# Waits on a pool's former bytes tile by tile, a bias copy from DRAM to DRAM, and the last tile's three pieces in three PSUM tiles

## The chip, the cores and the metric

The kernel runs on one core of one Trainium2 chip. The metric is the device time of one execution in microseconds (us), median of the runs shown; lower is better. The core's engines each have an instruction stream of their own: TensorE (PE; the loading of its weights is PEld), VectorE (DVE), ScalarE (ACT), GpSimd (POOL) and SyncE (SP). SP, ACT and POOL also issue DMAs. An engine works in the order of its stream, so an instruction that waits holds back all that stand behind it.

## The reference

One decoder layer for a prompt of 1024 tokens and a sample group of 8 × 8 tokens with 512 past tokens each:

```python
h = rms_norm(x, norm_mix);  z = h @ w_in          # q, three K/V branches, gates, 512 pooling channels
o_att  = nsa(q, gates, kv_cmp, kv_sel, kv_win)    # compressed, selected and window branch, per-head gates,
                                                  # all with a relative-position bias from rel_bias
o_pool = pool_mix(u)                              # trailing means over 2/4/8/16 positions minus the token,
                                                  # a linear map per group, a scale per channel
x = x + concat(o_att, o_pool) @ w_out
x = x + swiglu(rms_norm(x, norm_ffn));  y = rms_norm(x, norm_final)
```

All of it is in 32-bit floating point. The new cache rows are outputs too.

## The kernel before, in words

A product of two fp32 operands is made of three PE products: each operand is split into a high and a low part (`split`: ACT makes the high part as a cast, L163, DVE the low part as a difference, L164).

The stages, by the profile's time. Up to about 118 us: the norm, the first projection of 128-column units (`useq`), the four pooling units (`pool_unit`, `pool_mm`), the bias tables (`prep_bias`) and the gates. A unit's weight is loaded by SP into `wraw` (L210) and split two units ahead. To about 260 us: the other units (the next one after the pooling units is that of column 512), the compressed branch. To 650 us: attention, tile by tile, with the output projection as filling work. To 715: the entry of the feed-forward part. To 1151: its first product by a scheme of block sums (`pq`, L1405). To 1353 its second, and then `last_group`, which adds the last part of the second product to nine token tiles (eight of 128 rows, the sample tile of 64), and takes the final norm.

The order of instructions on an engine is found by a scheduler in the tile framework, from the program's text and its dependences; it is not written out by hand. Buffers come from pools. A pool opened where another was closed takes over bytes of the former one, and its first instructions wait for the former users.

`prep_bias` makes with two matmuls a table `bt` [8 heads, 751] in SBUF, 383 columns of near distances and 368 of compressed ones. ACT copies both out of PSUM and stores two forms to DRAM: `bd`, the table, and `br`, in which each head's 383 values stand 128 times, once for each partition (L430, L431). SP then loads `bnear` from `br` with a pitch that shifts each partition by one (L439), and the small tables `bcmp`, `bss` and `bsm` from `bd` (L443 to L449). POOL copies `bss` to `bsw` (L451). In the same stretch SP reads the page table `ptrow` into registers with 32 register loads (L1061), and `pool_mm` stores `oth` and `otl` to `odp` by POOL's DMAs (L403); `oth` and `otl` have two buffers each.

In `last_group` a tile's PSUM tile `pl` takes the transposed residual (L1644) and the products (L1659). DVE adds `y`, ACT squares it (L1671), a short chain makes the scale (L243 to L249), DVE multiplies and SP stores. The last tile is done in pieces of 512, 256 and 256 columns of one PSUM tile (L1663).

Of the kernel before, what the change touches and what calls it, by code (L numbers as in the profile page):

```python
# [10 lines left out]
F32 = mybir.dt.float32  # L11
# [3 lines left out]
OP = mybir.AluOpType  # L15
AX = mybir.AxisListType
PSUM = bass.MemoryType.PSUM
DRAM = bass.MemoryType.DRAM

D = 1024  # L20
# [3 lines left out]
NS = NB * TS  # L24
NT = T + NS
H = 8
# [17 lines left out]
L1 = 383  # L44
L3 = 16 * 23
# [29 lines left out]
class K:  # L75
# [6 lines left out]
    def pool(self, name, bufs=1, space=None, side=None, stack=None):  # L82
        kw = dict(name=name, bufs=bufs)
        if space is not None:
            kw["space"] = space
        if side is not None:
            kw["side"] = side
        return (stack or self.ctx).enter_context(self.tc.tile_pool(**kw))

    def run(self):  # L90
        self.cst = self.pool("cst")
        wps = ExitStack()
        self.wp = self.pool("wp", 2, stack=wps, side="right")
        self.dr = self.pool("dr", 1, DRAM)
        self.odp = [self.dr.tile([128, 4, NT], F32, name=f"odp{i}") for i in range(2)]
        self.odb = [self.dr.tile([128, 4, 128], F32, name=f"odb{i}") for i in range(8)]
        self.x2p = [self.dr.tile([128, D], F32, name=f"x2p{i}") for i in range(9)]
        self.x2t = [self.dr.tile([128, D], F32, name=f"x2t{i}") for i in range(9)]
        self.hdA = self.dr.tile([128, 8, HT], F32, name="hdA")
        self.hdB = [self.dr.tile([128, 8, n], F32, name=f"hdB{n}_{i}") for i, n in enumerate((160, 128, 128))]  # L100
        self.qd = self.dr.tile([8, 128, H, 128], F32, name="qd")
        self.gd = self.dr.tile([NS, 24], F32, name="gd")
        self.bd = self.dr.tile([H, L1 + L3], F32, name="bd")
        self.br = self.dr.tile([H, 128, 384], F32, name="br")
        self.td = [self.dr.tile([3, 8, 128, HT], F32, name=f"td{g}") for g in range(3)]
        self.tl = self.dr.tile([8, 128, HT], F32, name="tl")
        att = ExitStack()
        self.bp = self.pool("bias", 1, stack=att)
        proj = ExitStack()
        self.psd = self.pool("psd", 4, PSUM, stack=proj)  # L110
        self.pst = self.pool("pst", 4, PSUM, stack=proj)
        h1p = self.pool("h1", 1, stack=proj, side="right")
        self.consts()
        bts = ExitStack()
        self.btp = self.pool("bt", 1, stack=bts)
        with ExitStack() as s:
            self.norm1(self.pool("xn", 1, stack=s, side="right"), h1p)
        self.stg = self.pool("stg", 2, stack=proj, side="right")
        self.useq = [0] + [1304 + 128 * k for k in (3, 2, 1, 0)] + [512, 640, 128, 256, 384, 768, 1024, 896, 1152]
        self.ucur = self.w_split(self.w0)  # L120
        pbs = ExitStack()
        pp = self.pool("pb", 1, stack=pbs)
        self.q_unit(0)
        self.pool_setup(pp)
        bias = self.prep_bias()
        next(bias)
        mm = self.pool_mm(pp)
        for k in (3, 2, 1, 0):
            self.pool_unit(pp, k, (lambda: next(mm)) if k < 2 else None)
            next(bias, None)  # L130
        for _ in range(3):
            next(mm)
        self.gates()
        for _ in mm:
            pass
        pbs.close()
        bts.close()
        with ExitStack() as s:
            cp = self.pool("cp", 1, stack=s)
            self.cmp_units(cp)  # L140
            self.compress_setup(cp)
            cmp = self.compress(cp)
            next(cmp)
            for u in (1, 2, 3):
                self.q_unit(u, lambda: next(cmp))
        self.kvp = self.pool("kv", 1, stack=att)
        self.eps = ExitStack()
        self.ep = self.pool("ep", 1, stack=self.eps)
        self.units = [self.unit(i, g, pp) for i in map(int, '01276543') for g in range(2) for pp in range(2)]
        for n, u in enumerate(self.units):  # L150
            u["n"] = n
        early = self.early()
        self.kv_units(lambda: next(early, None))
        for _ in early:
            pass
        proj.close()
        wps.close()
        self.attention(att)
        self.ffn(att)
# [246 lines left out]
    def prep_bias(self):  # L406
        nc, I, cst, bi = self.nc, self.I, self.cst, self.bp
# [17 lines left out]
        for a, b in ((0, L1), (L1, L1 + L3)):  # L425
            ps = self.dp()
# [1 line left out]
            nc.scalar.copy(bt[:, a:b], ps[:H, :b - a])  # L428
        yield
        nc.scalar.dma_start(self.bd, bt)  # L430
        nc.scalar.dma_start(self.br[:, :, 0:L1], bt[:, 0:L1].unsqueeze(1).to_broadcast([H, 128, L1]))  # L431
        nc.sync.dma_start(wm8, I["wm8_c"])
        yield
        bd = self.bd
# [2 lines left out]
        def skew(offset, ap):  # L437
            return bass.AP(tensor=bd.tensor, offset=bd.offset + offset, ap=ap)
        nc.sync.dma_start(self.bnear[:, :, 64:320],  # L439
                          bass.AP(tensor=self.br.tensor, offset=self.br.offset + 127,  # L440
                                  ap=[[383, 128], [128 * 384, H], [1, 256]]))
        for a in range(8):
            nc.sync.dma_start(self.bcmp[16 * a:16 * a + 16, :, 48:64], skew(L1 + 7 - a, [[23, 16], [LT, H], [1, 16]]))  # L443
        for b2 in range(2):
# [1163 lines left out]
    def last_group(self, f0, lacts, s):  # L1608
# [3 lines left out]
        ws = []  # L1612
# [9 lines left out]
        gB = lp.tile([128, D], F32, name="gB")  # L1622
        gsrc = I["norm_final"]
        order = [(p, 128, b) for p, n, b in TILES if n == 128]
        order.insert(6, (512, NS, 8))
        ys = []
        for i, (p0, rows, b) in enumerate(order):
            ys.append(lp.tile([128, D], F32, name=f"y{i}"))
# [8 lines left out]
                for k in range(gn)]  # L1637
        for i, (p0, rows, b) in enumerate(order):
            final = i == len(order) - 1
            sl = self.qfree[i % 4]  # L1640
            ps = pss[sl].tile([128, D], F32, name=f"pl{sl}")
            for k in range(8):
                xk = xsm[:, k] if b == 8 else self.xs(k, p0, rows)
                nc.tensor.matmul(ps[:rows, 128 * k:128 * k + 128], xk, self.ident, is_transpose=True,  # L1644
                                 start=(k % 4 == 0), stop=False, skip_group_check=True)
            parts = ((0, 512), (512, 256), (768, 256)) if final else ((0, 512), (512, 512))
            y = ys[i][:rows]
            sq = lp.tile([128, D], F32, name="fsq", bufs=2)
            ss = lp.tile([128, 3], F32, name="fss", bufs=2)
            v = lp.tile([128, 1], F32, name="fv", bufs=2)[:rows]  # L1650
            r = lp.tile([128, 1], F32, name="fr", bufs=2)[:rows]
            t = lp.tile([128, 1], F32, name="ft", bufs=2)[:rows]
            for q, (c0, n) in enumerate(parts):
                cs = slice(c0, c0 + n)
                for k in range(gn):
                    a, l = [x[:, p0:p0 + rows] for x in flat[k]]
                    wh, wl = [w[:, cs] for w in ws[k]]
                    for j, (x, w) in enumerate(((a, wh), (a, wl), (l, wh))):
                        nc.tensor.matmul(ps[:rows, cs], x, w, start=False, stop=(k == gn - 1 and j == 2),  # L1659
                                         skip_group_check=True)  # L1660
                if not final:
                    continue
                nc.vector.tensor_tensor(y[:, cs], ps[:rows, cs], y[:, cs], op=OP.add)  # L1663
                nc.scalar.activation(sq[:rows, cs], y[:, cs], AF.Square, accum_out=ss[:rows, q:q + 1])
                if q == 0:
                    nc.vector.tensor_tensor(y[:, cs], y[:, cs], gB[:rows, cs], op=OP.mult)
                elif q == 1:
                    nc.vector.tensor_tensor(v, ss[:rows, 0:1], ss[:rows, 1:2], op=OP.add)
            if not final:
                nc.vector.tensor_tensor(y, ps[:rows], y, op=OP.add)  # L1670
                nc.scalar.activation(sq[:rows], y, AF.Square, accum_out=ss[:rows, 0:1])  # L1671
                self.rstd_ops(v, r, t, ss[:rows, 0:1])
                nc.vector.scalar_tensor_tensor(y, y, r, gB[:rows], op0=OP.mult, op1=OP.mult)
                dst = O["y_sample"].rearrange("b t d -> (b t) d") if b == 8 else O["y_prompt"][0, 128 * b:128 * b + 128]
                nc.sync.dma_start(dst, y)
                continue
            nc.vector.tensor_tensor(ss[:rows, 2:3], ss[:rows, 2:3], v, op=OP.add)
            self.rstd_ops(v, r, t, ss[:rows, 2:3])
            dst = O["y_prompt"][0, 128 * b:128 * b + 128]
            nc.scalar.activation(y[:, 0:512], y[:, 0:512], AF.Copy, scale=r)  # L1680
            nc.vector.scalar_tensor_tensor(y[:, 512:], y[:, 512:], r, gB[:rows, 512:], op0=OP.mult, op1=OP.mult)
            nc.scalar.dma_start(dst[:, 0:512], y[:, 0:512])
            nc.sync.dma_start(dst[:, 512:], y[:, 512:])
# [33 lines left out]
```

## Time and profile before

| | |
|---|---|
| runs | 1428.23, 1424.76, 1427.62 us; median 1427.62 |
| profiled execution | 1423.89 us; its span, first to last instruction, 1422.1 us |
| granted TensorE clock, mean | 0.985 |
| busy share of the span | PE 95%, DVE 68%, ACT 46%, POOL 15% |
| DMA | 172.71 MB, 121 GB/s in the mean |

In a row of the timeline stand: start, duration, engine, line, operation, output<-input, shapes, and in brackets how long the engine had stood idle and whose end released it. "ACTq", "SPq" and "POOLq" are the queues that issue DMAs. In the chain of work that ended last a row is start, length, what. A row of busy time by stage holds the stretch and its length, the busy time of PE, PEld, DVE, ACT and POOL, the granted clock (1.00 is full), the DMA engines' busy share and GB/s.

### The profile page before, as it was taken

Reading aid. Unit: us, or ns where it says so; the run is one execution under the profiler, and the core shown is the slowest. Engines: PE = TensorE matmul, PEld = TensorE weight load, DVE = VectorE, ACT = ScalarE, POOL = GpSimd, SP = SyncE. Lnnn points to the kernel's source line nnn. Section 1 sums busy time; section 2 is a strip of 40 time slices with the busy share of each in tenths; the row PEclk is TensorE's granted clock in tenths of the full one; section 3 lists DMA queues with packets and bytes.
Section 4 is the critical chain, followed back from the end, with each engine's and each line's share of the span. In section 5 each row is a group of like instructions: output and inputs, shape, how many; then the busy total and the mean of one; then the engine's idle time right before and its main releaser. Section 6 shows DMA issues by size and latency. Waiting matters only on the chain.

```text
span 1422.1 us, 25073 instructions
## 1 busy us (share of the span) xinstructions
PE 1351.1 (95%) x9326; PEld 1251.6 (88%) x9326; DVE 963.8 (68%) x2234; ACT 659.6 (46%) x1504; POOL 207.5 (15%) x354
## 2 busy tenths in 40 slices
PE   7979999889999989997799999999999999999997
PEld 6968999768878778875699999999999999999985
DVE  5655877777766688886975565565556475879744
ACT  7322445675665677765533333333333363525322
POOL 0124223432212223331000000000000010101000
PEclk9989999999999999999899999999999999999999
DMA  6457331445445232333332333332333262526251
GB/s 199 95 144 233 111 106 35 142 132 156 127 127 162 73 115 90 112 97 132 84 118 79 108 123 108 108 111 63 103 123 108 92 219 68 188 90 228 82 200 67
DMA packets 156261, 172.71 MB, mean 121 GB/s; under 512 B 19331, under 2 KB 122339, under 8 KB 155363
## 3 DMA queue, kind: packets, MB, share of 16 engines
q1 hardware_dynamic: 143363, 125.94, 29.0%
q0 software_dynamic: 11584, 43.31, 8.8%
q10 hardware_dynamic: 1192, 1.86, 1.0%
q8 instruction: 74, 1.21, 0.4%
q14 instruction: 48, 0.39, 0.1%
HBM read 113.35 MB, written 57.84 MB: 120 GB/s over the span
## 4 chain that ended last, share of the span: by engine, by line
PE 71%; DVE 8%; issue 8%; DMA 4%; ACT 4%; SPq 4%; POOL 1%; POOLq 0%; ACTq 0%; DVEq 0%
PE pq L1405 38%; PE dp L236 7%; PE tp L1013 4%; PE pl L1659 3%; SPq L1061 3%; PE dp L1199 2%; PE O L1037 2%; PE dp L1201 2%; PE O L1038 2%; PE dp L1200 2%; PE S L924 2%; PE S L925 2%; DMA r<-td 1%; DVE blP L164 1%; PE dp L1156 1%
## 5 line engine op out<-in xcount | busy, mean ns | idle before, releaser
L1405 PE MATMUL pq<-bhP,sh 128*128 128x272 f32 x1232 | 357.0, 290 | 9.2 <-ACT sh L163 4.3
L1405 PE MATMUL pq<-blP,sh 128*128 128x272 f32 x1232 | 357.6, 290 | 2.6 <-DVE blP L164 2.6
L1405 PE MATMUL pq<-bhP,sl 128*128 128x272 f32 x1232 | 356.3, 289 | 1.4 <-DVE sl L164 1.4
L1405 PEld LDWEIGHTS pq<-bhP,sh 128*128 128x128 f32 x1232 | 234.3, 190 | 10.5 <-ACT sh L163 5.0
L1405 PEld LDWEIGHTS pq<-blP,sh 128*128 128x128 f32 x1232 | 234.1, 190 | 3.3 <-DVE blP L164 3.3
L1405 PEld LDWEIGHTS pq<-bhP,sl 128*128 128x128 f32 x1232 | 234.2, 190 | 1.9 <-DVE sl L164 1.9
L1405 PE MATMUL pq<-r,sh 128*128 128x272 f32 x1008 | 190.8, 289 | 2.9 <-DVE blk L1477 2.8
L163 ACT CAST sh<-ws 128x512 fp32r<-128x512 f32 (+1 forms) x136 | 78.7, 583 | 206.2 <-PE pq L1405 137.9
L164 DVE TENSOR_TENSOR sl<-ws,sh 128x512 fp32r<-128x512 f32 (+1 forms) x136 | 86.6, 641 | 126.3 <-ACT sh L163 126.1
L1405 PEld LDWEIGHTS pq<-r,sh 128*128 128x128 f32 x1008 | 157.9, 189 | 3.7 <-issue 1.8
L1405 PE MATMUL pq<-r,sl 128*128 128x272 f32 x504 | 143.9, 286 | 0.0
L1022 DVE TENSOR_TENSOR pl<-tp,ph 128x512 fp32r<-128x512 f32 (+8 forms) x168 | 103.6, 621 | 43.8 <-ACT ph L1021 42.4
L163 ACT CAST sh<-wr 128x512 fp32r<-128x512 f32 (+1 forms) x102 | 59.1, 583 | 144.7 <-PE pq L1405 133.5
L1021 ACT CAST ph<-tp 128x512 fp32r<-128x512 f32 (+8 forms) x168 | 88.7, 533 | 65.2 <-PE tp L1013 55.2
L236 PE MATMUL dp<-h1h,whi 128*128 128x384 f32 (+1 forms) x336 | 113.1, 337 | 3.2 <-DVE ue L310 3.2
L236 PE MATMUL dp<-h1l,whi 128*128 128x384 f32 (+1 forms) x336 | 112.2, 334 | 0.0
L236 PE MATMUL dp<-h1h,wlo 128*128 128x384 f32 (+1 forms) x336 | 112.0, 333 | 0.0
L1586 POOL DMA_DIRECT2D r<-td x21 | 15.7, 750 | 602.9 <-PE pq L1405 583.3
L1405 PEld LDWEIGHTS pq<-r,sl 128*128 128x128 f32 x504 | 95.2, 189 | 0.0
L164 DVE TENSOR_TENSOR sl<-wr,sh 128x512 fp32r<-128x512 f32 (+1 forms) x102 | 65.0, 637 | 34.8 <-ACT sh L163 34.6
L1037 PE MATMUL O<-ph,vn 128*128 128x256 f32 x264 | 79.9, 317 | 6.5 <-ACT ph L1021 5.0
L1003 POOL TENSOR_SCALAR pwin<-pwin,r 128x640 f32<-128x640 f32 (+4 forms) x64 | 42.4, 666 | 247.1 <-DVE r L996 115.2
(343 smaller groups left out, 2982.2 us busy)
## 6 DMA issues: line engine op xcount, KB each, us to landing
wr<-in_w_ffn_in SPq DMA_DIRECT2D x44, 512.0 KB
td<-blk SPq DMA_DIRECT2D x18, 1088.0 KB
r<-td POOLq DMA_DIRECT2D x21, 816.0 KB, 6.1
wr<-in_w_ffn_out SPq DMA_DIRECT2D x48, 192.0 KB
wraw<-in_w_in SPq DMA_DIRECT2D x14, 512.0 KB
x<-in_x_prompt SPq DMA_DIRECT2D x8, 512.0 KB
qi<-qd SPq DMA_DIRECT2D x8, 512.0 KB
op<-odp SPq DMA_DIRECT2D x16, 256.0 KB
```

What stands on the lines that cost most here:

```text
L163: nc.scalar.copy(hi, src)
L164: nc.vector.tensor_tensor(lo, src, hi.bitcast(F32), op=OP.subtract)
L236: nc.tensor.matmul(ps, w[:, k, :], x, start=(k == 0 and j == 0), stop=(k == kt - 1 and j == 2))
L924: nc.tensor.matmul(S[:, c0:c0 + n], q, kh[:, k0:k0 + n], start=True, stop=False)
L1003: nc.gpsimd.tensor_scalar(t, t, r[:, hh, b:b + 1], 1.0, op0=OP.mult, op1=OP.mult)
L1013: nc.tensor.transpose(tp[:kk, 256 * x + 128 * hh:256 * x + 128 * hh + 128], u["P"][hh, b][:, kb * 128:kb * 128 + kk], self.ident)
L1021: nc.scalar.copy(ph[:kk, a:e], tp[:kk, a:e])
L1022: nc.vector.tensor_tensor(pl[:kk, a:e], tp[:kk, a:e], ph[:kk, a:e].bitcast(F32), op=OP.subtract)
L1037: nc.tensor.matmul(o, vv, ph[:kk, cs], start=(2 * t + x == 0), stop=False)
L1061: reg = nc.sync.value_load(self.ptrow[0:1, 4 * b + kb:4 * b + kb + 1], min_val=0, max_val=39)
L1405: nc.tensor.matmul(ps[:, c, :HQ], w[:, k], x[:, k, cs], start=(fresh and k == 0 and j == 0), stop=(k == kt - 1 and j == 2), skip_group_che ...
L1659: nc.tensor.matmul(ps[:rows, cs], x, w, start=False, stop=(k == gn - 1 and j == 2), skip_group_check=True)
```

## The change

Three edits. Each pool outside DRAM is opened with `reuse_waits="tile"`: a tile waits for the former users of the bytes that it takes itself, not for those of the whole former pool. In `prep_bias` the table `br` has another layout and is written by a DMA that POOL issues, from `bd` in DRAM, after `bd` has landed. In `last_group` the sample tile goes last, and the three pieces of the last tile are in three PSUM tiles.

```diff
         if side is not None:
             kw["side"] = side
+        if space != DRAM:
+            kw["reuse_waits"] = "tile"
...
-        self.br = self.dr.tile([H, 128, 384], F32, name="br")
+        self.br = self.dr.tile([128, H, 384], F32, name="br")
...
         nc.scalar.dma_start(self.bd, bt)
-        nc.scalar.dma_start(self.br[:, :, 0:L1], bt[:, 0:L1].unsqueeze(1).to_broadcast([H, 128, L1]))
+        bd, LT = self.bd, L1 + L3
+        nc.gpsimd.dma_start(self.br[:, :, 0:L1],
+                            bass.AP(tensor=bd.tensor, offset=bd.offset, ap=[[0, 128], [LT, H], [1, L1]]))
...
         nc.sync.dma_start(self.bnear[:, :, 64:320],
                           bass.AP(tensor=self.br.tensor, offset=self.br.offset + 127,
-                                  ap=[[383, 128], [128 * 384, H], [1, 256]]))
+                                  ap=[[H * 384 - 1, 128], [384, H], [1, 256]]))
...
-        order.insert(6, (512, NS, 8))
+        order.append((512, NS, 8))
...
-            sl = self.qfree[i % 4]
-            ps = pss[sl].tile([128, D], F32, name=f"pl{sl}")
+            parts = ((0, 512), (512, 256), (768, 256)) if final else ((0, D),)
+            pt = {}
+            for q, (c0, n) in enumerate(parts):
+                sl = self.qfree[(i + q) % 4]
+                pq = pss[sl].tile([128, D], F32, name=f"pl{sl}")
+                for c in range(c0, c0 + n, 128):
+                    pt[c] = pq[:, c - c0:c - c0 + 128]
+                pt[q, "all"] = pq[:rows, :n]
...
-                nc.vector.tensor_tensor(y[:, cs], ps[:rows, cs], y[:, cs], op=OP.add)
+                cs = slice(c0, c0 + n)
+                nc.vector.tensor_tensor(y[:, cs], pt[q, "all"], y[:, cs], op=OP.add)
...
-            dst = O["y_prompt"][0, 128 * b:128 * b + 128]
+            dst = O["y_sample"].rearrange("b t d -> (b t) d")
```

Line numbers of the changed kernel are 2 to 11 higher than before. The scheduler's order changes in three places. SP, from the weight `wraw` that stands between the register loads; `in_w_in` is the projection's weight in DRAM. Before:

```order
L210 DMA wraw<-in_w_in 128x8x128
...
L1061 TENSOR_LOAD ptrow
...
L439 DMA bnear<-br 128x8x256
L443 DMA bcmp<-bd 16x8x16 x8
L446 DMA bss<-bd 64x1x128
L448 DMA bsm<-bd 64x1x8 x2
L449 DMA bsm<-bd 64x1x7
L446 DMA bss<-bd 64x1x128
L448 DMA bsm<-bd 64x1x8 x2
L449 DMA bsm<-bd 64x1x7
L210 DMA wraw<-in_w_in 128x8x128 x2
```

and now:

```order
L212 DMA wraw<-in_w_in 128x8x128
L447 DMA bcmp<-bd 16x8x16 x8
L450 DMA bss<-bd 64x1x128
L452 DMA bsm<-bd 64x1x8 x2
L453 DMA bsm<-bd 64x1x7
L450 DMA bss<-bd 64x1x128
L443 DMA bnear<-br 128x8x256
L452 DMA bsm<-bd 64x1x8 x2
L453 DMA bsm<-bd 64x1x7
L1065 TENSOR_LOAD ptrow
...
L212 DMA wraw<-in_w_in 128x8x128
```

Ten of the 32 register loads stood between the first weight and the bias loads; now they stand behind, two of them ahead of the next weight and eight behind it. `bnear` is now behind the small tables.

ACT in the same stretch, from the copy of the first part of `bt` out of PSUM (`dp`); `nps`, `npp` and `ue` belong to a pooling unit. Before:

```order
L428 COPY bt<-dp 8x383
L431 DMA br<-bt 1024x1x383
L362 COPY nps<-tp 64x128
L363 COPY npp<-tp 15x128
L163 CAST plh<-pl 128x1088
L428 COPY bt<-dp 8x368
L350 COPY ue<-tp 128x8x15
L362 COPY nps<-tp 64x128
L363 COPY npp<-tp 15x128
L430 DMA bd<-bt 8x751
```

and now:

```order
L430 COPY bt<-dp 8x383
L430 COPY bt<-dp 8x368
L364 COPY nps<-tp 64x128
L365 COPY npp<-tp 15x128
L352 COPY ue<-tp 128x8x15
L432 DMA bd<-bt 8x751
L165 CAST plh<-pl 128x1088
```

The store of `bd` stands ahead of the cast of `plh`, and that of `br` is gone from ACT. POOL behind the stores `qd` of the queries; before:

```order
L673 DMA qd<-qb 128x2x128
L403 DMA odp_63<-oth 128x384
L403 DMA odp_64<-otl 128x384
L403 DMA odp_63<-oth 128x384
L403 DMA odp_64<-otl 128x384
L403 DMA odp_63<-oth 128x320
L451 COPY bsw<-bss 128x512
L403 DMA odp_64<-otl 128x320
L452 TENSOR_SCALAR bsw<-wm_527 128x8
```

and now:

```order
L677 DMA qd<-qb 128x2x128
L434 DMA br<-bd 1024x1x383
L455 COPY bsw<-bss 128x512
L456 TENSOR_SCALAR bsw<-wm_527 128x8
L405 DMA odp_63<-oth 128x384
L405 DMA odp_64<-otl 128x384
```

The copy `bsw`, which waits for the `bss` loads, now stands ahead of all stores of `oth` and `otl`. Elsewhere up to `last_group` the order is the same or nearly so; what changes there are the waits. For the feed-forward entry: the first `blk<-hdA` (L1502) waited for `op` (L164) and waits now for a reciprocal and a transpose of the last attention tile; the load `xr<-in_w_out` of the chain at 508 us waited for a matmul beside it and now waits for an earlier one.

More of the change, by code (lines that the diff above doesn't have):

```diff
@@ L1639, in last_group @@
             final = i == len(order) - 1
-            sl = self.qfree[i % 4]
-            ps = pss[sl].tile([128, D], F32, name=f"pl{sl}")
+            parts = ((0, 512), (512, 256), (768, 256)) if final else ((0, D),)
[6 more added lines that the diff above has]
+                pt[q, "all"] = pq[:rows, :n]
             for k in range(8):
                 xk = xsm[:, k] if b == 8 else self.xs(k, p0, rows)
-                nc.tensor.matmul(ps[:rows, 128 * k:128 * k + 128], xk, self.ident, is_transpose=True,
-                                 start=(k % 4 == 0), stop=False, skip_group_check=True)
-            parts = ((0, 512), (512, 256), (768, 256)) if final else ((0, 512), (512, 512))
+                nc.tensor.matmul(pt[128 * k][:rows], xk, self.ident, is_transpose=True,
+                                 start=(k % 4 == 0 or (final and k == 6)), stop=False, skip_group_check=True)
             y = ys[i][:rows]
@@ L1653, in last_group @@
             for q, (c0, n) in enumerate(parts):
[L1654 to L1660, printed above, removed]
+                for b0 in range(0, n, 512):
+                    e0 = min(n, b0 + 512)
+                    for k in range(gn):
+                        a, l = [x[:, p0:p0 + rows] for x in flat[k]]
+                        wh, wl = [w[:, c0 + b0:c0 + e0] for w in ws[k]]
+                        for j, (x, w) in enumerate(((a, wh), (a, wl), (l, wh))):
+                            nc.tensor.matmul(pt[q, "all"][:, b0:e0], x, w, start=False,
+                                             stop=(k == gn - 1 and j == 2), skip_group_check=True)
                 if not final:
                     continue
-                nc.vector.tensor_tensor(y[:, cs], ps[:rows, cs], y[:, cs], op=OP.add)
+                cs = slice(c0, c0 + n)
+                nc.vector.tensor_tensor(y[:, cs], pt[q, "all"], y[:, cs], op=OP.add)
                 nc.scalar.activation(sq[:rows, cs], y[:, cs], AF.Square, accum_out=ss[:rows, q:q + 1])
@@ L1669, in last_group @@
             if not final:
-                nc.vector.tensor_tensor(y, ps[:rows], y, op=OP.add)
+                nc.vector.tensor_tensor(y, pt[0, "all"], y, op=OP.add)
                 nc.scalar.activation(sq[:rows], y, AF.Square, accum_out=ss[:rows, 0:1])
@@ L1673, in last_group @@
                 nc.vector.scalar_tensor_tensor(y, y, r, gB[:rows], op0=OP.mult, op1=OP.mult)
-                dst = O["y_sample"].rearrange("b t d -> (b t) d") if b == 8 else O["y_prompt"][0, 128 * b:128 * b + 128]
-                nc.sync.dma_start(dst, y)
+                nc.sync.dma_start(O["y_prompt"][0, 128 * b:128 * b + 128], y)
                 continue
```

## The prediction

> **What bounds the kernel now.** I read the page's busy times first, then busy time by stage, then the timeline and the chain that ended last inside the stages where TensorE (PE) is not full.
>
> ```profile
> PE 1351.1 (95%) x9326; PEld 1251.6 (88%) x9326; DVE 963.8 (68%) x2234; ACT 659.6 (46%) x1504; POOL 207.5 (15%) x354
> 88.00:118.00 30.00, 22.21 (x108) 17.49 (x109) 20.32 (x37) 10.08 (x22) 9.21 (x17) 0.77 0.57 163
> 118.00:260.00 142.00, 139.80 (x895) 136.52 (x894) 101.89 (x277) 59.23 (x169) 46.75 (x82) 1.00 0.36 109
> 650.00:715.00 65.00, 45.61 (x250) 39.54 (x248) 50.73 (x79) 31.96 (x43) 2.73 (x5) 0.84 0.40 123
> 715.00:1151.00 436.00, 436.00 (x3480) 436.00 (x3481) 252.44 (x372) 151.84 (x251) 3.76 (x5) 1.00 0.34 106
> 1353.00:1422.00 69.00, 59.01 (x302) 47.44 (x300) 32.50 (x78) 15.78 (x37) 0.00 (x0) 0.98 0.39 138
> ```
>
> The stage rows give length, then busy time of PE, weight loads, DVE, ACT and POOL, the granted clock, the DMA share and GB/s. PE carries the kernel, so only time in which PE waits or runs at a lowered clock can be won. It is lost in 88–118 (clock 0.77), 650–715 and the last 12 us. From 118 to 260 and from 715 to 1151 PE is all but full, so what is won ahead of these stages reaches the end. The change touches all three weak places.
>
> **Term A, the start (50–118 us).** These rows are from the chain, the timeline, the DMA answer for 49–83 us, and, in its last row, the page's DMA queues.
>
> ```profile
> 48.84 1.29 ACTq L431 DMA_DIRECT2D br<-bt  x1
> 49.80 0.26 SPq L1061
> 50.36 1.96 SPq L1061
> ...
> 79.90 1.86 SPq L1061
> q10 hardware_dynamic: 1041, 1.59, 41.4%
> 63.92 0.40 SPq L210 DMA_DIRECT2D wraw<-in_w_in  x1
> 84.36 5.79 DMA bnear<-br
> 86.69 1.04 ACT L163 CAST whi<-wraw 128x1024 fp32r<-128x1024 f32 x1 [10.35 <-DMA wraw<-in_w_in]
> 88.20 0.55 DVE L400 SCALAR_TENSOR_TENSOR otl<-dp,psc,oth 128x320 fp32r<-128x320 f32 x1 [10.07 <-ACT oth L399]
> 84.81 6.13 SPq L443 DMA_DIRECT2D bcmp<-bd  x8
> 93.67 2.16 DMA bss<-bd
> 69.09 0.58 POOL L403 DMA_DIRECT2D odp<-oth  x1 [22.75 <-ACT oth L399]
> 95.96 0.61 POOL L451 COPY bsw<-bss 128x512 f32<-128x512 f32 x1 [6.96 <-DMA bss<-bd]
> 96.20 1.02 SPq L210 DMA_DIRECT2D wraw<-in_w_in  x2
> 101.87 1.04 ACT L163 CAST whi<-wraw 128x1024 fp32r<-128x1024 f32 x1 [5.04 <-DMA wraw<-in_w_in]
> 102.33 0.62 DVE L400 SCALAR_TENSOR_TENSOR otl<-dp,psc,oth 128x384 fp32r<-128x384 f32 x1 [4.61 <-DMA odp<-otl]
> 85.87 0.34 PE L236 MATMUL dp<-h1h,wlo 128*128 128x384 f32 x1
> 117.93 0.34 PE L236 MATMUL dp<-h1h,whi 128*128 128x384 f32 x1
> q0 software_dynamic: 11584, 43.31, 8.8%
> ```
>
> The copy br<-bt reads 1024 rows out of 8 partitions. ACT's queue (q10) is busy with it from 49 to 83 us. While it runs, each register load of the page table on SP (L1061) takes 1.9 us instead of 0.26; sixteen of them cost about 26 us more than before 50. Behind them SP issues everything late: the weight of 63.92, the bias loads of 84.81, the weights of 96.20. ACT, which works in order, stands 10.35 us at the cast of that weight, which PE needs only at 117.93, and 5.04 us at the next. DVE stands 10.07 us behind ACT, and 4.61 us for an odp store that queued on POOL behind the copy bsw, itself waiting for bss.
>
> In the changed order ACT has both bt copies together and the bd store right behind them: issued at about 51, landed at about 53 (the small DMA bss took 2.16). POOL then issues br from bd. SP has about three register loads left at 50, so the first weight goes at about 52.5 instead of 63.92. The eight bcmp loads follow at 53, the last bss at about 62, and bnear waits for br. bsw is copied at about 65, before POOL's first odp store (now at 69.09), so placing bsw ahead of all odp stores costs nothing as long as bss lands by then.
>
> How long T the copy br<-bd takes is shown nowhere. Bounds: bnear moved two thirds of these bytes in 5.79 us; br<-bt took about 33. POOL's queue had 11,584 packets in 8.8% of 16 × 1422.1 us, which is 0.173 us a packet; 1024 rows on 16 engines are 64 each, so 11 us. I take 11, since that row is the same queue. [...]
>
> With T = 11, br lands at about 65, the weight of 96.20 goes at about 69 and lands 5.67 later (96.20 to 101.87), long before ACT asks for it (101.87 − 5.04 − 10.35 = 86.5). So the two ACT waits and both DVE waits end: 10.07 + 4.61 = 14.7 us of DVE standing still. The ceiling is PE: from 86.2 to 117.93 lie 31.7 us, in which the work at full clock is about 22.21 × 0.77 = 17.1 us, so at most 14.6. DVE has 20.32 us of work there and hands over to ACT and PE several times; it could go on at 78.1 instead of 88.20, and end at 98.5 plus its hand-overs, so some 4 us of small gaps stay. A = −11 (bounds −14.6 and, with T = 33, below).
>
> **Term B and C, waits of loads.** With waits tile by tile, the load of the first output weight at 260 us may go up to 0.5 us earlier. The second stands on the chain:
>
> ```profile
> 508.07 3.68 DMA xr<-in_w_out
> ```
>
> This load waited for a matmul of the former user of its pool; now it is free some 5 us earlier. Of its 3.68 us only what no other work covers is won, and ACT, DVE and PE all have work of this stage beside it. B and C: −0.3 and −0.6 (0 to −1.5 together; −3.68 at the very most for C).
>
> **Term D, the entry of the feed-forward part.**
>
> ```profile
> 660.20 0.43 PE tp L1013 x2
> 664.66 0.69 DVE L164 TENSOR_TENSOR op<-of,op 128x512 fp32r<-128x512 f32 x1 [0.68 <-ACT op L163]
> 665.81 0.32 SPq L1502 DMA_DIRECT2D blk<-hdA  x1
> 671.09 2.01 ACT L163 CAST bhP<-blk 128x2176 fp32r<-128x2176 f32 x1 [6.46 <-DMA blk<-hdA]
> 671.83 0.69 DVE L1273 TENSOR_TENSOR xr<-dp,xr 128x512 f32<-128x512 f32 x1 [2.53 <-PE dp L1201]
> 673.13 2.42 DVE L164 TENSOR_TENSOR blP<-blk,bhP 128x2176 fp32r<-128x2176 f32 x1 [0.60 <-ACT bhP L163]
> 675.48 8.75 DMA wr<-in_w_ffn_in
> 670.00:680.00 10.00, 5.86 (x23) 4.67 (x22) 7.50 (x12) 6.09 (x6) 0.58 (x1) 0.77 1.07 352
> 690.00:700.00 10.00, 6.70 (x52) 6.28 (x50) 10.00 (x7) 7.13 (x7) 0.00 (x0) 0.97 0.00 0
> ```
>
> The first blk load waited for op (664.66), the last piece of work in the pools whose bytes it takes. Now it waits for its own bytes' users, a softmax division and a transpose of the group that ended at 660.63, so it goes about 5 us earlier than 665.81. The second blk and the weights behind it still wait for op and gain about 1.4. But blP stands on DVE behind the add of 671.83, which no load delays, so it comes 0.6 earlier. After that DVE is the bound: full from 690, with 2.5 us free in 670–680. Between −0.6 and −0.6 − 2.5 = −3.1 I take −1.5, near the earlier weights' 1.4.
>
> **Term F, the last tile.**
>
> ```profile
> 1410.10 0.68 DVE L1663 TENSOR_TENSOR y<-pl,y 128x512 f32<-128x512 f32 x1
> 1410.84 0.39 PE L1659 MATMUL pl<-wkh,la 128*128 128x256 f32 x1 [2.19 <-DVE y L1663]
> 1411.62 0.69 DVE L1666 TENSOR_TENSOR y<-y,gB 128x512 f32<-128x512 f32 x1 [0.84 <-ACT fsq L1664]
> 1413.05 1.69 PE pl L1659 x12
> 1414.76 0.42 DVE L1663 TENSOR_TENSOR y<-pl,y 128x256 f32<-128x256 f32 x1 [1.03 <-PE pl L1659]
> ```
>
> PE waits for DVE's adds because all pieces share a PSUM tile. With three tiles PE goes straight on after the 512 piece, which ended at 1410.84 − 2.19 = 1408.65: 1408.65 + 2 × 1.69 = 1412.0 instead of 1413.05 + 1.69 = 1414.74. On DVE the 512 add stays at 1410.10, since DVE is at the tile before until then; the add of the second piece follows at 1410.8, the multiply at 1411.62, ending at 1412.3; the sum of ACT's first two squares, which I allow 0.4 us, and then the third add at about 1412.7 instead of 1414.76. F = −2.1 (bounds 0 and −2.7). Having the sample tile last halves the rows of the final stores, not the columns that DVE and PE walk; 0 for that.
>
> **Sum.** −11 − 0.3 − 0.6 − 1.5 − 2.1 = −15.5 on an execution of 1423.89 (its span 1422.1), so 1408.4 there. The median of the three runs is 1427.62, 3.7 above the profiled one; against it 1412. About 0.3%, 4.3 us, is what a measurement of this kernel can tell from no change.
>
> **Rivals.** *Half of the start.* With T about 33, br lands at 87; the three bsm loads and two register loads behind bnear on SP (about 3 us) and 5.67 us for the weight put ACT's second cast at about 96.5 instead of 101.87. A = −5.4, sum −9.9: 1417.7. For it: 33 us is the only time seen for these rows. Against: bnear and the q0 row.
>
> *The start gives nothing.* The weight issued at 52.5 shares the engines with br. Before, the one issued at 63.92 took 22.7 us (to 86.69) beside it. If br holds all engines until 87, the weight lands there, ACT's 10.35 us wait stays, and B to F leave −4.5: 1423. [...]
>
> *Slower.* Rows of one small DRAM area are read 128 times and written; if T passes about 39 us, the second cast is later than 101.87, and each further us costs one. Beyond T = 48 it outweighs the other terms by 4.3. At T = 55 the sum is +11: 1439. Against it: no copy of this size in the trace took over 33 us, and the q0 row.
>
> *The waits by tile do nothing.* Without B, C and D the sum is −13.1: 1414.5, inside the forecast.
>
> **Chances.** The forecast (1406 to 1415) 0.63; half of the start 0.18; the start gives nothing 0.10, split evenly over the 0.3% line; slower 0.06; the rest, 0.03, a gain over 22 us. Faster 0.86 by these, which I lower to 0.84 for stages that could give time back; same 0.10, slower 0.06. The range reaches from the full bounds (−14.6, −1.5, −3.1, −2.7: −21.9) to past the half case: 1405 to 1421.
>
> **What would show it.** A: register loads at 0.3 to 0.6 us after 50, the two casts without long waits, PE's first matmul of unit 512 near 107, the clock near 1 there. C, D: the loads 5 us earlier, little else. F: no wait of PE in the last tile. I am wrong if br<-bd takes over 30 us or holds the weight that ACT needs, or if a later stage waits by as much as the start gains.

## The result, and the profile after

| | before | after |
|---|---|---|
| median of the runs shown together | 1427.92 us | 1404.12 us (1402.17 to 1408.70) |
| ratio, 95% interval | | 0.9839 [0.9809, 0.9870] |
| profiled execution | 1423.89 us | 1408.70 us |
| measured again, with the parts | 1425.70 us | 1403.08 us; 0.9833 [0.9817, 0.9850] |
| profiled execution of the second measurement | | 1403.82 us |

The changed kernel is about 23 us faster. The forecast was 1412 with a range from 1405; the first median lies 0.9 us below that range, the second 1.9.

The page of the changed kernel, first part, and its busy time by stage (the columns are those of the stage rows above):

```profile
PE 1349.5 (96%) x9326; PEld 1253.6 (89%) x9326; DVE 963.4 (68%) x2234; ACT 658.8 (47%) x1504; POOL 209.8 (15%) x355
90.00:95.00 5.00, 4.34 (x26) 2.93 (x25) 4.72 (x9) 2.04 (x4) 2.78 (x6) 1.00 0.54 180
95.00:100.00 5.00, 4.61 (x32) 3.16 (x30) 2.98 (x6) 2.26 (x4) 1.50 (x3) 1.00 0.91 247
633.00:697.00 64.00, 46.82 (x248) 40.75 (x246) 50.18 (x78) 31.41 (x42) 2.73 (x5) 0.81 0.41 127
1137.00:1339.00 202.00, 198.22 (x1545) 197.35 (x1546) 153.59 (x227) 84.16 (x128) 12.72 (x17) 0.98 0.43 140
```

PE does the same work; what went is idle time. At the start PE now runs at the full clock, with 0.66 and 0.39 us of waiting in 90–100. The entry of the feed-forward part (633–697) is as weak as before.

The start of the changed kernel, from the register loads' group (durations min/median/max in ns), the page's DMA issues (KB, us from issue to landing) and the timeline (start, length, in brackets the wait and what ended it):

```profile
L1065 SPq TENSOR_LOAD <-ptrow x32: 262/278/787, 38.5 to 75.3; - x32
br<-bd POOLq DMA_DIRECT2D x1, 1532.0 KB, 9.3
51.48 0.88 POOL L434 DMA_DIRECT2D br<-bd  x1 [6.19 <-DMA bd<-bt]
52.88 0.39 SPq L212 DMA_DIRECT2D wraw<-in_w_in  x1
67.61 0.75 POOL L455 COPY bsw<-bss 128x512 f32<-128x512 f32 x1 [15.25 <-DMA bss<-bd]
70.17 10.12 SPq L212 DMA_DIRECT2D wraw<-in_w_in  x2
74.52 1.05 ACT L165 CAST whi<-wraw 128x1024 fp32r<-128x1024 f32 x1 [2.79 <-PE dp L238]
88.22 1.05 ACT L165 CAST whi<-wraw 128x1024 fp32r<-128x1024 f32 x1 [2.73 <-PE dp L238]
91.14 0.38 PE L468 MATMUL dp<-h1h,gwhl 128*48 128x384 f32 x1 [0.66 <-DVE otl L402]
106.82 0.56 DVE L312 TENSOR_TENSOR zs<-dp,rB 128x384 f32<-128x384 f32 x1 [0.24 <-PE dp L238]
```

and the last of these instructions in the timeline of before:

```profile
122.32 0.56 DVE L310 TENSOR_TENSOR zs<-dp,rB 128x384 f32<-128x384 f32 x1 [0.24 <-PE dp L236]
```

The copy takes 9.3 us from issue to landing. No register load takes over 0.79 us. The weights go at 52.88 and from 70.17 instead of 63.92 and 96.20, and ACT's two casts wait for PE, no longer for a DMA. The first result of unit 512 (`zs`) is 15.5 us earlier.

The two other places:

```profile
643.55 0.32 SPq L1506 DMA_DIRECT2D blk<-hdA  x1
648.35 0.33 SPq L1508 DMA_DIRECT2D blk<-hdA  x1
648.74 2.01 ACT L165 CAST bhP<-blk 128x2176 fp32r<-128x2176 f32 x1 [1.14 <-DMA blk<-hdA]
654.77 0.69 DVE L1277 TENSOR_TENSOR xr<-dp,xr 128x512 f32<-128x512 f32 x1 [2.52 <-PE dp L1205]
655.38 2.42 DVE L166 TENSOR_TENSOR blP<-blk,bhP 128x2176 fp32r<-128x2176 f32 x1
1397.21 1.01 DVE L1674 TENSOR_TENSOR y<-pl,y 64x512 f32<-64x512 f32 x2
1398.20 0.28 PE L1669 MATMUL pl<-wkh,la 128*64 128x256 f32 x1
1399.41 0.41 DVE L1674 TENSOR_TENSOR y<-pl,y 64x256 f32<-64x256 f32 x1
```

At the feed-forward entry `bhP` no longer waits 6.46 us for the load, but 1.14; `blP` follows right behind the add of `xr`, as foreseen. In the last tile PE has ended before the third add, and waits for nothing.

### The profile page after: what moved, and what is told of

Read it like the earlier page. It is cut to its first block, busy times and chain, and to the rows that moved or that the text cites. A ratio compares the mean times of both kernels' runs of the same rounds, so it can differ in the third digit from the quotient of the medians.

```text
span 1406.9 us, 25024 instructions
## 1 busy us (share of the span) xinstructions
PE 1349.5 (96%) x9326; PEld 1253.6 (89%) x9326; DVE 963.4 (68%) x2234; ACT 658.8 (47%) x1504; POOL 209.8 (15%) x355
## 4 chain that ended last, share of the span: by engine, by line
PE 58%; issue 24%; DVE 9%; DMA 4%; ACT 4%; POOL 0%; SPq 0%; ACTq 0%; POOLq 0%; DVEq 0%
PE pq L1409 19%; PE dp L238 11%; PE tp L1017 4%; PE pl L1669 3%; PE dp L1203 2%; PE O L1041 2%; PE dp L1205 2%; PE dp L1204 2%; PE O L1042 2%; PE S L928 2%; PE S L929 2%; DMA r<-td 1%; DVE pl L1026 1%; DVE blP L166 1%; PE dp L1160 1%
## 5 line engine op out<-in xcount | busy, mean ns | idle before, releaser
L1026 DVE TENSOR_TENSOR pl<-tp,ph 128x512 fp32r<-128x512 f32 (+8 forms) x168 | 103.7, 622 | 42.8 <-ACT ph L1025 41.4
L1590 POOL DMA_DIRECT2D r<-td x21 | 15.7, 750 | 606.9 <-PE pq L1409 585.9
```

What stands on the lines that cost most here:

```text
L1026: nc.vector.tensor_tensor(pl[:kk, a:e], tp[:kk, a:e], ph[:kk, a:e].bitcast(F32), op=OP.subtract)
```

## The experiments

**The parts, alone and in pairs.** Each of these kernels has one or two of the three edits; the diffs are pieces of the change's.

Only `br` (the second edit):

```diff
+        nc.gpsimd.dma_start(self.br[:, :, 0:L1],
+                            bass.AP(tensor=bd.tensor, offset=bd.offset, ap=[[0, 128], [LT, H], [1, L1]]))
```

> Edit: only the second edit (br from bd by POOL, new layout); pools and last tile as before. Theory S (start): the whole of the start's gain is this edit's, since the changed kernel's profile has unit 512 about 15.5 us earlier; so 15 to 16 us less than before, ratio 0.989. Theory P (pools): a large part of the measured 23.8 us comes from the waits by tile, so this edit gives 8 to 12 us, ratio 0.992 to 0.994.

Measured: 1412.60 against 1425.70, ratio 0.9897 [0.9878, 0.9916]: 14.7 us less by the ratio, 13.1 by the medians. Theory S (0.989) lies in the interval, theory P (from 0.992) does not.

Only the waits by tile:

```diff
+        if space != DRAM:
+            kw["reuse_waits"] = "tile"
```

> Edit: only the first edit (waits by tile). Theory S: the loads at 508 and at 666 us go earlier, worth 1 + 0.6 us as in the profile of the changed kernel, so 1 to 3 us less, ratio 0.998 to 0.999; register loads stay at 1.9 us. Theory P: 6 to 10 us less, ratio 0.993 to 0.996.

Measured: 1426.38, ratio 1.0001 [0.9986, 1.0015]: nothing that can be told. Theory P is out; of theory S only the weak end, 0.999, lies in the interval.

Only the last tile:

```diff
-        order.insert(6, (512, NS, 8))
+        order.append((512, NS, 8))
...
+                sl = self.qfree[(i + q) % 4]
```

> Edit: only the third edit (sample tile last, three PSUM tiles). Both theories: no wait of PE in the last tile, 2 to 2.5 us less, ratio 0.9983. A third theory, that the sample tile's place delays something in the second feed-forward product, has 0 or a loss.

Measured: 1422.92, ratio 0.9970 [0.9954, 0.9986]: 4.3 us less by the ratio, 2.8 by the medians.

All three, on the same chip:

> The changed kernel once more, on the same chip as the three parts. Theory S: the parts add up, 15.5 + 1.6 + 2.2 = 19 to 20 us less than before (ratio 0.986), and what the first measurement showed above that (23.8) is the spread of the runs before. If the ratio is again 0.984 and the parts sum to 19 or less, the parts help each other.

Measured: 1403.08, ratio 0.9833 [0.9817, 0.9850]: 23.8 us by the ratio, 22.6 by the medians. The three parts give 14.7 − 0.1 + 4.3 = 18.9 by the ratios. So theory S had the start right, but the parts do not quite add up: 4.9 us are missing, and the four intervals together leave about 4.7 (an estimate that takes them as independent), so this is barely clear of noise. That asked for the pairs.

The first and second edit, without the last tile's (the runs of the kernel before that stand beside this and the following pair have a median of 1424.71):

> Edit: the first and second edit without the third. In the profiles so far, the time from the add of the last full tile to the end was 17.1 us before, 19.4 and 18.7 with the first or the second edit alone (there the clock was halved for a part of the last tile), and 14.7 to 14.8 in all three profiles with the third edit. Theory G (PE's waits in the last tile can also halve the clock, by the phase in which they fall): this kernel is 2.4 to 4.7 us slower than the changed one, ratio to before 0.9855 to 0.987. Theory N (no such effect): 2.4 us slower, 0.985.

Measured: 1408.96, ratio 0.9879 [0.9849, 0.9909]: 6.6 us slower than the changed kernel by the two ratios, further than either theory had. The interval reaches both theories, so the time does not decide between them; the profile below does.

The second and third, without the waits by tile:

> Edit: the second and third edit, pools as before. The profiles put the waits by tile at about 0.6 (to 305) + 0.8 (at 525) + 2 (650 to 715) won and 1.2 lost (at 1137), so 2 us net: ratio 0.985 to 0.986, 2 us slower than the changed kernel. If the waits by tile bring nothing, as their measurement alone says (ratio 1.0001), it is equal to the changed kernel, 0.983 to 0.984.

Measured: 1407.44, ratio 0.9864 [0.9837, 0.9892]: 4.4 us slower than the changed kernel by the two ratios, where the waits by tile alone had given nothing. The interval reaches both cases here too, so what this edit is worth in the median stays open.

Here is the length of each stage in the one profile of each kernel (us), cut at an instruction that all have: the first `zs` of unit 512, POOL's `pwin` at 525 (of before), ACT's `op` at 664, ACT's `u` at 714 and at 1153, DVE's add of the last full tile, the end.

| kernel | to zs | 525 | 664 | 714 | 1153 | 1405 | end |
|---|---|---|---|---|---|---|---|
| before | 122.3 | 403.1 | 139.3 | 50.3 | 438.7 | 251.4 | 17.1 |
| br only | 105.8 | 403.3 | 140.4 | 52.2 | 439.0 | 250.7 | 19.4 |
| waits by tile only | 121.7 | 401.1 | 139.2 | 49.7 | 439.8 | 254.8 | 18.7 |
| last tile only | 121.6 | 403.5 | 139.2 | 52.4 | 438.8 | 251.7 | 14.7 |
| br and waits | 105.7 | 401.3 | 139.3 | 49.7 | 439.9 | 251.3 | 18.8 |
| br and last tile | 106.1 | 404.4 | 139.6 | 52.3 | 438.8 | 249.6 | 14.8 |
| all, first profile | 106.8 | 400.7 | 140.1 | 49.6 | 439.9 | 254.9 | 14.8 |
| all, second profile | 106.8 | 401.1 | 139.9 | 49.7 | 440.0 | 249.7 | 14.8 |

The columns tell the edits apart better than the totals do. `br` takes 15.5 to 16.5 us from the start. Between kernels that differ in them alone, the waits by tile take 2.0 to 3.7 us up to 525 and 0.6 to 2.7 at the feed-forward entry (column 714), and cost 0.9 to 1.3 up to 1153. These three are weak evidence: the six kernels of the next part, all without the waits by tile, have 401.7 to 403.7 in the column 525, only 0.4 above the highest with them (401.3), and 438.9 to 439.9 in the column 1153. The last-tile edit makes the end 14.7 or 14.8 us in every profile, against 17.1 or 18.7 to 19.4.

That the end has two lengths without it is the clock. The wait of PE in the last tile, from the timeline of the kernel with `br` and waits, and the stage row behind it:

```profile
1393.06 0.39 PE L1663 MATMUL pl<-wkh,la 128*128 128x256 f32 x1 [2.19 <-DVE y L1667]
1395.00:1400.00 5.00, 3.03 (x13) 2.64 (x12) 1.32 (x5) 1.05 (x5) 0.00 (x0) 0.50 0.00 0
```

and the stage row at the same place of before:

```profile
1410.00:1415.00 5.00, 3.36 (x24) 2.96 (x24) 2.31 (x6) 1.24 (x4) 0.00 (x0) 1.00 0.27 108
```

PE's wait is 2.19 us in both, yet in the kernel with `br` and waits the granted clock falls to 0.50 behind it, and in the profile of before it stays at 1.00. Without the last-tile edit the end is 18.7 to 19.4 us long in four profiles (three of the table, and the DRAM copy by ACT with heads outermost below, 19.0), and 17.1 or 17.2 in before and the other five kernels below; with the edit it is 14.7 or 14.8 in all four.

The granted clock changes only at steps of 3.41 us: in the profiles of before and of the changed kernel the stretches between one change and the next are whole multiples of 3.413 us, from 1 (105.45 to 108.87 of before, at 0.50) to 209. Cut at these steps, the wait lies whole in one step in the kernel with `br` and waits, where PE is busy for 1.22 of 3.41 us,

```profile
1390.79:1394.20 3.41, 1.22 (x10) 1.15 (x10) 2.50 (x5) 0.72 (x2) 0.00 (x0) 1.00 0.28 114
```

and is cut in two in the profile of before, where PE is busy for 2.70 and 1.69:

```profile
1405.95:1409.36 3.41, 2.70 (x12) 1.85 (x10) 1.69 (x8) 1.35 (x3) 0.00 (x0) 1.00 0.00 0
1409.36:1412.77 3.41, 1.69 (x12) 1.49 (x12) 2.32 (x4) 0.72 (x2) 0.00 (x0) 1.00 0.40 159
```

All ten profiles without the last-tile edit divide so. In the four with the long end PE stands for 2.18 to 2.20 us of one step, and the clock falls at the end of that step; in the other six the wait is cut, PE stands for at most 1.75 us of any step that holds a part of it, and the clock stays until PE is done. So a standstill of 2.18 us within one step was enough here, less than the whole step. No run moved the wait on purpose.

**What made the start slow.** Six kernels that vary the copy `br`: its length, its queue, its source, its layout and the place of the table in SBUF; one profile of each.

An eighth of the repeats:

```diff
-        nc.scalar.dma_start(self.br[:, :, 0:L1], bt[:, 0:L1].unsqueeze(1).to_broadcast([H, 128, L1]))
+        nc.scalar.dma_start(self.br[:, 0:16, 0:L1], bt[:, 0:L1].unsqueeze(1).to_broadcast([H, 16, L1]))
...
-                                  ap=[[383, 128], [128 * 384, H], [1, 256]]))
+                                  ap=[[0, 128], [128 * 384, H], [1, 256]]))
```

> Edit on the kernel before: br<-bt writes 16 of the 128 repeats (an eighth of the bytes, still from bt in SBUF, by ACT), and bnear reads row 0 for all partitions; this leaves out the shift of the near bias. SP's and ACT's order stays. Theory O (the time that br<-bt is in flight): it ends at about 53 instead of 83, register loads are back at 0.3 to 0.6 us from there, the casts of 86.69 and 101.87 wait little, unit 512 starts 12 to 15 us earlier (its first zs at 107 to 110 instead of 122.3). Theory R (the loads are slow whatever br does, and only their place in SP's order counts): loads stay at 1.9 us, zs at 120 or later.

Measured: 1407.27 in one run against 1427.54; the first `zs` at 106.65. This kernel leaves out the shift of the near bias and serves the timing alone.

```profile
L1061 SPq TENSOR_LOAD <-ptrow x32: 262/271/1960, 39.0 to 62.0; - x32
62.60 0.37 SPq L439 DMA_DIRECT2D bnear<-br  x1
88.08 1.05 ACT L163 CAST whi<-wraw 128x1024 fp32r<-128x1024 f32 x1 [2.74 <-PE dp L236]
```

With SP's order of before, all loads still ahead of the bias tables, the whole gain of the start is there (15.7 us). Two loads are still slow, 1.24 and 1.96 us at 49.5 and 51.0, while the short copy runs; the others behind them take 0.26 to 0.46. Theory O holds, theory R falls: the long copy was the cost, not the order.

From SBUF as before, but issued by POOL:

```diff
-        nc.scalar.dma_start(self.br[:, :, 0:L1], bt[:, 0:L1].unsqueeze(1).to_broadcast([H, 128, L1]))
+        nc.gpsimd.dma_start(self.br[:, :, 0:L1], bt[:, 0:L1].unsqueeze(1).to_broadcast([H, 128, L1]))
```

> Edit on the kernel before: br<-bt from SBUF as before, but issued by POOL; the scheduler then puts the eight bcmp, bss and bsm ahead of the register loads on SP, as in the changed kernel. Theory O: br still takes about 30 us and the register loads beside it 1.9 us each, but the weight and the bias loads go ahead of them, so zs at 108 to 112. If ACT's queue and not the SBUF source was slow, br takes about 10 us on POOL's queue and the loads 0.3 to 0.6 us.

Measured: 1433.06 in one run, 5.5 us slower than before; `zs` at 131.98.

```profile
br<-bt POOLq DMA_DIRECT2D x1, 1532.0 KB, 35.0
L1061 SPq TENSOR_LOAD <-ptrow x32: 262/272/1959, 38.4 to 98.5; - x32
86.93 1.04 ACT L163 CAST whi<-wraw 128x1024 fp32r<-128x1024 f32 x1 [15.92 <-DMA wraw<-in_w_in]
```

A miss: I had 108 to 112. POOL's queue does not make the copy faster, it takes 35.0 us, and the weight beside it is as late as before. Only five slow register loads stand ahead of that weight here, and it goes at 60.56 instead of 63.92, yet ACT gets it at 86.93 as against 86.69, 26.4 us after its issue, where the weight of 96.20 in the profile of before took 5.67; so the copy delays the weight in flight beside it too, and not through the slow loads alone. Part of the slowdown is another order of the `oth` and `plh` that the scheduler chose here, so this kernel's time is no clean price; the copy's 35.0 us is.

From DRAM by POOL, heads outermost, and from DRAM by ACT, new layout:

```diff
+        nc.gpsimd.dma_start(self.br[:, :, 0:L1],
+                            bass.AP(tensor=bd.tensor, offset=bd.offset, ap=[[LT, H], [0, 128], [1, L1]]))
```

> Edit on the kernel before: br from bd in DRAM by POOL, but in the former layout, heads outermost (8) on both sides instead of 128 partitions. If a copy spreads over as many engines as divide the outermost dimension, it runs on 8 and takes about 18 us (the changed kernel's 9.3 us doubled). Register loads beside it: 0.3 to 0.6 us if the SBUF source slowed them, 1.9 if it is 8 engines filled with br. zs at 106 to 109.

Measured: the copy takes 12.3 us, not 18; no load over 0.78 us; 1424.26 in one run, `zs` at 118.88, not 106 to 109. It has the same other order of `oth` as the kernel before it, and PE waits for `otl`, so its time is no measure of the copy:

```profile
96.73 0.69 PE L236 MATMUL dp<-plh,wph 128*128 128x384 f32 x1 [6.54 <-DVE otl L400]
```

```diff
+        nc.scalar.dma_start(self.br[:, :, 0:L1],
+                            bass.AP(tensor=bd.tensor, offset=bd.offset, ap=[[0, 128], [LT, H], [1, L1]]))
```

> Edit on the kernel before: br from bd in DRAM in the new layout, but issued by ACT. ACT stands about 2 us until bd has landed (it has nothing due until 57), br takes 9 to 10 us as on POOL's queue, zs at 106 to 107: the queue does not count. If POOL's queue was what helped, br takes 20 us or more.

Measured: 1407.44 in one run, `zs` at 105.85, as expected. ACT's queue has moved all 1056 packets by 60 us, at most 9.7 us after the issue of the copy at 50.26. The queue does not count (9.3 us by POOL), the source does (33 us by ACT and 35.0 by POOL out of SBUF).

The same with heads outermost:

```diff
+        nc.scalar.dma_start(self.br[:, :, 0:L1],
+                            bass.AP(tensor=bd.tensor, offset=bd.offset, ap=[[LT, H], [0, 128], [1, L1]]))
```

> Edit on the kernel before: br from bd in DRAM, heads outermost (8), issued by ACT; with m3 (16 engines, 128 outermost, ACT) it differs in the layout alone. If the outermost dimension of 8 confines a copy of this queue to 8 engines, br takes about twice m3's time and the DMA share is half while it runs; if not, the same. Register loads beside it stay at 0.26 to 0.8 us if the SBUF source slowed them before.

Measured: 1414.26 in one run, `zs` at 107.18. Two of its register loads fall beside the copy, and are not slow (the loads' group and ACT's queue in 51.2 to 52.2 us):

```profile
L1063 SPq TENSOR_LOAD <-ptrow x2: 262/267/272, 51.2 to 51.8; - x2
q10 hardware_dynamic: 91, 0.14, 38.9%
```

In the kernel of before the first load beside the copy, at 50.36, took 1.96 us. These two loads, and one at 51.9 in the preceding kernel (0.26 us), are few, but they say that it is the source in SBUF that slows the loads, not a copy on this queue as such.

The copy of before, out of partitions 64 to 71 (`rb` is widened to 64 + H columns, with zeros ahead):

```diff
-        bt = self.btp.tile([H, L1 + L3], F32, name="bt")
+        bt = self.btp.tile([64 + H, L1 + L3], F32, name="bt")[64:64 + H]
...
-            nc.tensor.matmul(ps[:H, :b - a], rb, oh[:, a:b], start=True, stop=True)
-            nc.scalar.copy(bt[:, a:b], ps[:H, :b - a])
+            nc.tensor.matmul(ps[:64 + H, :b - a], rb, oh[:, a:b], start=True, stop=True)
+            nc.scalar.copy(bt[:, a:b], ps[64:64 + H, :b - a])
```

> Edit on the kernel before: the table bt is made in partitions 64 to 71 instead of 0 to 7 (the matmul gets 72 columns, 64 of them zero); everything else as before, br<-bt by ACT from SBUF. The page table that SP's register loads read lies in partition 0. If br takes 33 us because one partition's reads feed each of 8 engines, it stays at about 33. If the loads are slow since they read SBUF at the same place as br, they are at 0.3 to 0.6 us now and SP is on time (zs about 12 us earlier, unless the weight beside br is late); if they are slow since the DMA engines are taken, they stay at 1.9 us and zs at 122.

Measured: 1425.89 in one run, `zs` at 123.08.

ACT's DMA queue in 52 to 57 us (packets, MB, share of the 16 engines' time), of before:

```profile
q10 hardware_dynamic: 162, 0.25, 43.7%
```

out of DRAM by ACT with heads outermost:

```profile
q10 hardware_dynamic: 522, 0.80, 45.8%
```

and with 128 outermost:

```profile
q10 hardware_dynamic: 893, 1.37, 100.2%
```

At the same share of the engines DRAM gives 522 packets where SBUF gave 162: 0.070 us a packet against 0.216 (share × 80 us / packets). 128 outermost then fills all engines, 100.2% against 45.8% with 8 outermost, on this queue; the gain is 893 packets against 522, 1.7 times and not twice. On POOL's queue it was 9.3 us against 12.3. With the table in partitions 64 to 71 the row of 52–57 is that of before to the last digit, and the loads stay slow:

```profile
L1062 SPq TENSOR_LOAD <-ptrow x32: 262/553/2296, 38.6 to 80.6; - x32
84.90 0.37 SPq L440 DMA_DIRECT2D bnear<-br  x1
```

So it is not that they read the same partitions. Whether the copy is slow because its source is in SBUF or because it spans only 8 partitions was not tried.

## Why the prediction was wrong

The step that failed is the size of term A, forecast −11 and measured −15.5; smaller shares come from the last tile's clock and from the step from profile to median. The steps, against the second profile of the changed kernel (its span is 20.1 us shorter than that of before; forecast 15.5):

- **Term A, forecast −11, measured −15.5.** Mechanism, place and order of events were right, by the first profile, in which `zs` stands within 0.01 us of the second: T was 9.3 (forecast 11), the weight went at 52.88 (52.5), `bsw` was copied at 67.61 (65), the next weight from 70.17 (69). The term was mis-sized by two things. I left "some 4 us of small gaps" for hand-overs; there were 0.66 + 0.39 us, since PE now has matmuls queued while DVE and ACT hand over: the two casts wait 2.79 and 2.73 us for PE, and not PE for them. From PE's last matmul of 85.87 on (it stands at 83.95 now), 13.6 us of the ceiling of 14.6 went. And the ceiling counted only from there: 1.9 us went ahead of that point, where PE had waited too (1.15 us for `pll` at 67.56), so the ceiling itself was too low, and with it the lower end of the range.
- **B and C, forecast −0.9.** From `zs` to 525 the second profile has another −2.0; the kernels that differ only in the waits by tile show 2.0 to 3.7 there. The term was too small, and its bound of −1.5 too; it is right in kind, as far as the spread of that column lets one tell.
- **Not forecast: +0.6 up to 664.** That column lies between 139.1 and 140.4 in all kernels; no edit stands out in it.
- **D, forecast −1.5.** −0.6 in this profile, −2.6 between kernels that differ in this edit alone (br with last tile against all). The second figure goes with the clock. Without the waits by tile the stage took 50.1 to 50.3 us in four profiles and 52.2 to 52.5 in six; in the six, and in no other, a step of half clock lies some 24 us behind `op`. With the waits by tile it took 49.6 or 49.7 in all four, none with that step. The rows of that place, of br with last tile (`op` at 650) and of br with waits (`op` at 646):

```profile
665.00:675.00 10.00, 7.22 (x48) 7.00 (x47) 8.49 (x16) 5.51 (x8) 0.00 (x0) 0.84 0.64 166
665.00:675.00 10.00, 9.46 (x77) 9.25 (x76) 10.00 (x13) 9.54 (x11) 0.00 (x0) 1.00 0.00 1
```

So 0.4 to 0.6 us are the edit's at the same clock; whether it also keeps that step away, or four profiles missed it by chance, stays open.
- **Not forecast: +1.3 up to 1153.** All kernels with the waits by tile have 439.8 to 440.0 there, but one without them, the copy by POOL from SBUF, has 439.9 too. Why was not found.
- **Not forecast: −1.6 up to 1405.** That stage is 249.6 to 254.9 us long in kernels with the same instructions there. The first profile of the changed kernel lost 5.2 us in it:

```profile
1270.20 0.79 PE L1409 MATMUL pq<-r,sh 128*128 128x272 f32 x2 [2.54 <-DVE blk L1481]
1270.00:1275.00 5.00, 4.80 (x21) 4.83 (x22) 3.73 (x6) 2.82 (x5) 0.09 (x1) 0.50 0.39 160
```

and the second, at the same place, did not:

```profile
1268.14 0.49 PE L1409 MATMUL pq<-r,sh 128*128 128x272 f32 x2 [0.70 <-DVE blk L1481]
1270.00:1275.00 5.00, 5.00 (x42) 5.00 (x41) 4.99 (x6) 3.94 (x4) 2.31 (x4) 1.00 0.78 268
```

- **F, forecast −2.1, measured −2.3** against the profile of before; 4.0 to 4.6 against profiles in which the clock fell there. The prediction took the waits as 2.19 + 0.52 us and gave the clock behind them no price.

From profile to median: the runs before lie 1.8 us (1425.70 − 1423.89) above their profile in the second measurement and 4.0 in the first, those after 0.7 below theirs. I had subtracted the terms from the median as if each run lost what the profiled one did. 20.1 + 1.8 + 0.7 = 22.6, the measured difference of the medians; why other runs lie above or below the profiled one was not traced.

Of the rivals, none came true. Half of the start and the start that gives nothing rested on T = 33, the slower one on T above 48; T was 9.3, near the q0 row (11) and away from the old copy's 33, because that was a matter of the source. That 11 came so near is in part luck. It took 1024 packets of 0.173 us on 16 engines; POOL's queue in 52 to 57 us of the changed kernel, where it carries this copy alone, shows

```profile
q0 software_dynamic: 242, 1.11, 77.4%
```

so 0.256 us a packet, but 4.6 KB in each, three rows: some 341 packets and 5.5 us of every engine (an estimate from this row), and the rest of T ahead of them and behind. That the waits by tile do nothing is what their own measurement says (1.0001), but the stage table shows a gain of some 3 us in it that the columns 1153 (1.1 us), 1405 (3.4) and end (1.6, the clock) take back in that profile.

Two slips of the working changed nothing: the sixteen loads took 28.6 us where the sixteen before them took 6.1, so some 22.6 more and not 26; and the chances of a faster kernel add up to 0.89, not 0.86.

## What to carry to other kernels

When a small table has to be repeated many times, look where the copy reads: here a copy out of 8 SBUF partitions held 41.4% of the DMA engines' time for some 34 us, with a weight beside it landing after 22.7 us and not 5.67, and the way out was to store the table once and replicate it from DRAM with 128 outermost. Follow a late queue back to the first instruction in it that has become slow; here 16 register loads hid a copy on another engine's queue. Here a wait of TensorE of 2.18 to 2.20 us had a second price, a clock of 0.50 behind it and an end of 18.7 to 19.4 us instead of 17.1 or 17.2, where it fell whole into one step of the clock; a single profile may not show it, and a change that takes such a wait away can gain more in the median than that profile says.

## What the runs showed of the hardware

- A copy of 1532 KB out of 8 SBUF partitions moved 50 GB/s in 52 to 57 us on either queue (some 33 us in all by ACT, 35.0 by POOL), out of partitions 0 to 7 as out of 64 to 71; out of DRAM the same bytes took 8.8 to 9.3 us by POOL with 128 outermost, and 12.3 with 8.
- A register load from SBUF took 0.26 us at the least, and up to 1.96 us (2.30 with the table in partitions 64 to 71) while such a copy was in flight. Beside a copy out of DRAM three loads took 0.26 to 0.27, and no load of a kernel that copies out of DRAM took over 0.79. How the copy out of SBUF slows it stays open.
- The granted clock changed only at steps of 3.41 us (1 to 209 of them between changes in the profiles of before and after). The same wait of 2.18 to 2.20 us was followed by a fall to 0.50 in the four profiles in which it lay whole in one step, and by none in the six in which it was cut.
